# New addresses in a partition for the weights' halves and the attention and convolution outputs of a hybrid decoder layer

## The chip, the core and the metric

The kernel runs on one core of a Trainium2 chip. The metric is the time of one execution on the device, in microseconds (us); the time before is the median of three runs. The engines are called PE (TensorE, matmuls), PEld (its weight loads), DVE (VectorE), ACT (ScalarE), POOL (GpSimd) and SP (SyncE, which here only issues transfers).

## The reference, cut to what matters

One decoder layer, 16 meta tokens and 512 tokens, width 2048, in float32. Each of the four matrix stages below is a product over 2048 or 5632 rows.

```python
n = _rmsnorm(h, g_mix[l])
p = n @ w_in[l]                                   # 2048 x 6144
q, k, v, gb, gc, u = jnp.split(p, ...)
o_attn = _stick_breaking_attention(q, k, v)       # 8 heads of 128
o_conv = gb * _causal_dwconv(gc * u, conv_w[l])   # 1024 channels
o = jnp.concatenate([_rmsnorm(o_attn, ...), _rmsnorm(o_conv, ...)], axis=-1)
h = h + o @ w_out[l]                              # 2048 x 2048
n2 = _rmsnorm(h, g_ffn[l])
h = h + (jax.nn.silu(n2 @ w_gate[l]) * (n2 @ w_up[l])) @ w_down[l]   # 5632 wide
```

The meta tokens' rows are dropped at the end.

## The kernel before

**Split operands.** A float32 product is made of three matmuls in the type fp32r: each operand is split in a high part (a rounded copy) and a low part (what is left), and the sum is high x high + high x low + low x high. So for each tile of 128 rows of the contraction (a k tile, counted by k) there are three matmuls in a row, at lines 168, 170 and 172 in the input projection, 662 to 664 in the output projection (`wide_product`) and 676 to 678 in the feed-forward part (`block_product`). The weights are the stationary operand (128x128), the activations the moving one (512, 264, 258 or 256 columns).

**Stages in order.** (1) Input projection, with attention woven into it head by head, then eight convolution groups; its weight halves `whi`, `wlo` are in the pool wpool. At the end of a head, ACT and DVE write the head's output as two halves, `oah` and `oal` (pool oapool, at the left end of memory); at the end of a convolution group `och` and `ocl` (pool ocpool, right above it). (2) Output projection, 16 tiles of 16 k tiles, 48 matmuls each, moving operands `oa` and `oc` of 512 columns; but for the first tile its weights are split into `s`. (3) Gate and up: 44 pairs, made from seven block products each in place of eight (a scheme that forms sums and differences of quarters of the operands); a block product has 8 k tiles, 24 matmuls of 256 columns. Its moving operands are the seven activation blocks `f0` to `f6` (tiles of the helper `slot`, in pools fpool and fpool_last). (4) Down projection: 32 pairs in four chunks of 5, 6, 5 and 6 k tiles, again seven block products per pair; its moving operands are 12 ring slots (`ring_tile`: `r0` to `r6`, and five slots in the tile `rest`), loaded by POOL from DRAM (`fd`), where stage 3 stored them (line 852).

**Weights in stages 2 to 4.** SP loads quarters into the tiles `b11`, `b12`, `b21`, `b22` (in stage 2 under the name `wide`), DVE forms sums `t1` to `t3`, and `split_quad` (line 591: ACT writes the high part; line 592: DVE the low one) fills one of three tiles `s`, [128, 2, 1024]. All of these are in the pool `sw`, allocated from the right end of memory below the pool hpool, which holds one tile, `acc_h`.

**Order and waits.** Each engine works through its own instructions in the order of the program; a matmul waits by semaphore for the halves that it reads. Pools are stacks from the left or right end of a partition's memory. They are opened with `reuse_waits="tile"`: a tile placed over a released pool waits for the old tiles that it overlaps, each as a whole.

**Addresses before.** All below are bytes modulo 256 within a partition, as they come out of the pools' sizes. `s`, `b`, `t` and `acc_h` start at 224, as `whi` and `wlo` do; `f0` to `f6` and all ring slots start at 240 (`slot` leaves 16 bytes at the front of a tile that starts at 224); `oah`, `oal`, `och` and `ocl` start at 224. The input projection's moving operands `nh` and `nl` start at 224, 32, 96 and 160 in turn, and are read from there, from 1056 bytes on (two halves of 264 columns), from 48 bytes on (258 columns), or from 64 bytes on (512 columns). Within a tile the k tiles follow each other at 512 bytes for weights, and at 1024 bytes for `f` and the rings.

Of the kernel before, what the change touches and what calls it, by code (L numbers as in the profile page):

```python
# [9 lines left out]
F32 = mybir.dt.float32  # L10
F32R = mybir.dt.float32r
# [4 lines left out]
P = 128  # L16
D = 2048
SEQ = 512
# [14 lines left out]
def hybrid_layer(ctx: ExitStack, tc: tile.TileContext, xT, w_in, w_out, w_gu, w_down, vecs, out):  # L33
# [250 lines left out]
    oapool.tile([P, 8], F32, name="pad_oa")  # L284
    acc_c = oapool.tile([P, SEQ], F32, name="acc_c")
    acc_a = oapool.tile([P, SEQ], F32, name="acc_a")
    oa = []

    def halves(ps, n):
# [67 lines left out]
    def attend(h, kn, kh, kl, qn, qh, ql, vt):  # L357
# [98 lines left out]
        def mix(ws):  # L456
            o = small(f"o{h}")
            for b in range(3):
                kk, q0 = slice(b * P, (b + 1) * P), Q0[b]
                th, tl = ws[b]  # L460
                pe.matmul(o[:, q0:], vh[:, kk], th, start=b == 0, stop=False)
                pe.matmul(o[:, q0:], vh[:, kk], tl, start=False, stop=False)
                pe.matmul(o[:, q0:], vl[:, kk], th, start=False, stop=False)
            pe.matmul(o[:, Q0[3] :], v32[:, :P], lw[:, 1184:1328], start=False, stop=False)
            pe.matmul(o[:, Q0[4] :], v32[:16, P:], lw[:16, 1328:1344], start=False, stop=True)
            g = g_att[:, h : h + 1]
            oh = oapool.tile([P, SEQ], F32R, name=f"oah{h}")
            ol = oapool.tile([P, SEQ], F32R, name=f"oal{h}")
            sc.activation(oh, o, AF.Copy, scale=g)
            ve.scalar_tensor_tensor(ol, o, g, oh.bitcast(F32), ALU.mult, ALU.subtract)  # L470
            square_sum(acc_a, o, h == 0)
            oa.append((oh, ol))
# [28 lines left out]
    for j in range(HEADS):  # L501
        pc = pp.tile([P, 2, 512], F32, tag="pp", name=f"pc{j}")
        product([(pc[:, 0, :CH], C0, C0 + CH), (pc[:, 1, :CH], C0 + CH, L)], n_hl)
        cu = t512(2 * CH, "e", 2)[:, : 2 * CH]
        ve.tensor_tensor(two(cu), halves(pc, CH), two(r2[:, C0:]), ALU.mult)
        pu = pp.tile([P, 2, 512], F32, tag="pp", name=f"pu{j}")
        product([(pu[:, 0, :CH], C0, C0 + CH), (pu[:, 1, :CH], C0 + CH, L)], n_hl)
        ve.tensor_tensor(two(cu), halves(pu, CH), two(cu), ALU.mult)
        y = t512(SEQ, "e2", 2)[:, :SEQ]
        sc.activation(y, cu[:, 2 : 2 + SEQ], AF.Copy, scale=cw[:, 3 * j : 3 * j + 1])  # L510
        for t in (1, 2):
            ve.scalar_tensor_tensor(
                y, cu[:, 2 + t : 2 + t + SEQ], cw[:, 3 * j + t : 3 * j + t + 1], y, ALU.mult, ALU.add
            )
        pb = pp.tile([P, 2, 512], F32, tag="pp", name=f"pb{j}")
        product([(pb[:, 0, :], META, L)], n_hl)
        gb = t512(SEQ, "v", 2)[:, :SEQ]
        ve.tensor_tensor(gb, pb[:, 0, :], r[:, META:], ALU.mult)
        gp.tensor_tensor(y, y, gb, ALU.mult)
        g = g_cnv[:, j : j + 1]  # L520
        if j == 0:
            assert not waiting
            after(10, scale_a)
            apool.release()
            ocpool = open_pool("ocpool")
        oh = ocpool.tile([P, SEQ], F32R, name=f"och{j}")
        ol = ocpool.tile([P, SEQ], F32R, name=f"ocl{j}")
        sc.activation(oh, y, AF.Copy, scale=g)
        ve.scalar_tensor_tensor(ol, y, g, oh.bitcast(F32), ALU.mult, ALU.subtract)
        square_sum(acc_c, y, j == 0)  # L530
        oc.append((oh, ol))
# [18 lines left out]
    hpool = open_pool("hpool", side="right")  # L550
    sw = open_pool("sw", side="right")
    acc_h = hpool.tile([P, SEQ], F32, name="acc_h")
    pairs = []
    def gate_up(f):
        return 8, [w_gu[n, f, k] for k in range(2) for n in range(2)]
# [160 lines left out]
    fpool = open_pool("fpool", side="right")  # L716
    hbuf = open_pool("hbuf", side="right")

    def slot(pool, dt, n, tag, name, gap=64):

        t = pool.tile([P, 2 * n * T2 + gap], dt, tag=tag, name=name)
        return t[:, 4 : 4 + 2 * n * T2].rearrange("p (a k t) -> p a k t", a=2, k=n)

    def pad(pool):
        pool.tile([P, 8], F32, name=f"pad_{pool.name}")

    acts = {i: slot(fpool, F32R, 8, f"f{i}", f"f{i}") for i in (0, 1, 2, 5)}
    fx = {i: dram.tile([P, 2, 8, T2], F32R, name=f"fx{i}") for i in (3, 4, 6)}
    for _ in range(4):
        load_wide()  # L730
# [11 lines left out]
    for i, j in enumerate(OUT_TILES):  # L742
# [32 lines left out]
        if i == KT - 1:  # L775
            with tc.high_priority(1 << 20):
                residual(ve)
                square_sum(acc_h, hj, False, wide_tmp("s"))
                mixed_blocks()
            ocpool.release()  # L780
            oapool.release()
            fp = open_pool("fp")
            rings_p = [open_pool("ring_0")]
            pad(rings_p[0])
            rings, n_ring, rest = {}, [0], []

            def ring_tile(dt, name):
                i = n_ring[0] % 12
                n_ring[0] += 1
                if i < 7:  # L790
                    return slot(rings_p[0 if i == 0 else 1 if i < 6 else 2], dt, 6, f"r{i}", name)
                if not rest:
                    rest.append(rings_p[2].tile([P, 5 * 12 * T2 + 16], F32R, name="rest"))
                t = rest[0][:, 4 : 4 + 5 * 12 * T2].rearrange("p (s a k t) -> p s a k t", s=5, a=2, k=6)
                return t[:, i - 7]

            r0 = ring_tile(F32R, "r0_0")
            fpool_last = open_pool("fpool_last")
            for s, n in ((3, 7), (4, 7), (6, 8)):
                acts[s] = slot(fpool_last, F32R, 8, f"f{s}", f"f{s}")  # L800
                for part in range(2):
                    gp.dma_start(acts[s][:, part, :n], fx[s][:, part, :n], max_dma_last_dim=4096)
            split_f(3, 6)
            split_f(4, 7)
        else:
            residual(gp if half else ve)
            if half:
                split_f(5, 2)
                st = hbuf.tile([P, 2, 2, T2], F32R, tag="st", name=f"st{j}")[:, :, 0]
                split(st[:, 0], st[:, 1], src[:, 3])  # L810
                gp.dma_start(fx[6][:, :, k], st)
            else:
                mixed_blocks()
                st = hbuf.tile([P, 2, 2, T2], F32R, tag="st", name=f"st{j}")
                split(st[:, 0], st[:, 1], src[:, 6:8])
                for n, s in enumerate((3, 4)):
                    gp.dma_start(fx[s][:, :, k], st[:, :, n])
# [56 lines left out]
    def load_acts(c, s):  # L874
        if c < len(CHUNKS):
            n = CHUNKS[c]
            rings[c, s] = (ring_tile(F32R, f"r{c}_{s}") if c or s else r0)[:, :, :n]

            for part in range(2):
                gp.dma_start(rings[c, s][:, part], fd[c][s][:, part], max_dma_last_dim=3072)  # L880
# [19 lines left out]
    rings_p.append(open_pool("ring_a", side="right"))  # L900
    for s in range(1, 6):
        load_acts(0, s)
    gate(FT - 1, g1, u1, x)
    apool.release()
    fpool_last.release()
# [3 lines left out]
    for c in range(len(CHUNKS)):  # L909
        end = c == len(CHUNKS) - 1  # L910
        if end:
            hh = ring_tile(F32, "hh")
        for j in range(KT // 2):

            if 1 <= j <= 5:
                load_acts(c + 1, j - 1)
            c1 = cpool.tile([P, 2, T2], F32, tag="c1", name=f"d1_{c}_{j}")
            c2 = cpool.tile([P, 2, T2], F32, tag="c2", name=f"d2_{c}_{j}")
            if end:
                h2 = [hh[:, :, 2 * (j % 3) + m] for m in range(2)]  # L920
                for m in (1, 0):
                    gp.dma_start(h2[m], two(hs[2 * j + m]))
            x = pair_product([rings[c, s] for s in range(7)], c1, c2)
            if j == KT // 2 - 1:
                for s in (5, 6):
                    load_acts(c + 1, s)
            if end:
                gp.tensor_tensor(c2, c2, h2[1], ALU.add)
                gp.tensor_tensor(c2, c2, r_h, ALU.mult)
                nc.sync.dma_start(two(out[2 * j + 1]), c2)  # L930
                ve.tensor_tensor(c1[:, 0], c1[:, 0], h2[0][:, 0], ALU.add)
                ve.tensor_tensor(c1[:, 0], c1[:, 0], r_h[:, 0], ALU.mult)
                ve.tensor_tensor(c1[:, 1], x, h2[0][:, 1], ALU.add)
                ve.tensor_tensor(c1[:, 1], c1[:, 1], r_h[:, 1], ALU.mult)
                nc.sync.dma_start(two(out[2 * j]), c1)
            else:
                sc.copy(c1[:, 1], x)
                gp.dma_start(two(hs[2 * j + 1]), c2, accum_op=ALU.add)
                gp.dma_start(two(hs[2 * j]), c1, accum_op=ALU.add)
# [61 lines left out]
```

## Time and profile before

| | |
|---|---|
| runs, median (lowest to highest) | 2148.52 us (2145.52 to 2150.7) |
| profiled execution, its own time | 2144.11 us |
| its span, first to last instruction | 2142.4 us |
| TensorE's mean granted clock | 0.996 of 2.4 GHz |

Stages in that span: input projection with attention and convolution to 629 us, output projection to 803, gate and up to 1686, down projection to the end. A profile is one execution; "busy" for an engine is time in which an instruction of its own runs, and a matmul's end is modelled, so matmuls overlap in the records and the distance between their starts says more than their durations.

### The profile page before, as it was taken

What the parts mean: (1) busy time and instruction counts of PE and PEld (TensorE: products, weight loads), DVE (VectorE), ACT (ScalarE), POOL (GpSimd) and SP (SyncE); (2) the same over time, 40 slices, a digit from 0 to 9 for tenths busy, and PEclk for the clock granted to TensorE, in tenths of its full rate; (3) what the DMA queues carried; (4) which work ended last, traced back from release to release, by engine and by line L of the source; (5) the groups of instructions that cost most, each with busy time, mean ns of one, the idle gap of its engine ahead of it and who ended that gap; (6) DMA issues with size and microseconds to landing.
All of it is one profiled execution on the core that took longest, in us unless ns stands there. A gap on an engine that the chain in (4) does not pass through costs nothing.

```text
span 2142.4 us, 39382 instructions
## 1 busy us (share of the span) xinstructions
PE 2109.6 (98%) x16086; PEld 2031.4 (95%) x16086; DVE 1644.2 (77%) x2131; ACT 1020.4 (48%) x1576; POOL 458.6 (21%) x584
## 2 busy tenths in 40 slices
PE   8999999999999998999999999999999899999999
PEld 7999999999988888999999999999999899999999
DVE  8777777434337778898888888888889777777798
ACT  6666565322224434554445455445445444444443
POOL 4111111101014453221211211211111323121222
PEclk9999999999999999999999999999999999999999
DMA  5222222232235556555555655655555999788763
GB/s 171 79 80 70 79 78 76 84 99 89 94 127 178 177 163 226 170 176 178 176 168 153 175 166 153 182 158 153 168 152 147 310 261 302 181 248 223 225 186 113
DMA packets 146005, 342.48 MB, mean 160 GB/s; under 512 B 13392, under 2 KB 58960, under 8 KB 145824
## 3 DMA queue, kind: packets, MB, share of 16 engines
q1 hardware_dynamic: 67824, 214.33, 31.6%
q0 software_dynamic: 78000, 125.63, 21.6%
q8 instruction: 126, 2.06, 0.4%
q14 instruction: 55, 0.45, 0.1%
HBM read 268.60 MB, written 71.30 MB: 159 GB/s over the span
## 4 chain that ended last, share of the span: by engine, by line
PE 91%; DMA 4%; DVE 3%; issue 1%; ACT 1%; POOL 0%; SPq 0%; DVEq 0%; ACTq 0%
PE x L676 11%; PE x L678 11%; PE x L677 10%; PE z L676 5%; PE z L678 5%; PE z L677 5%; PE y L678 3%; PE y L677 3%; PE y L676 3%; PE po L662 3%; PE po L663 3%; PE po L664 3%; DMA b<-w_down 2%; PE pv L168 1%; PE pu L172 1%; PE pc L172 1%
## 5 line engine op out<-in xcount | busy, mean ns | idle before, releaser
L591 ACT CAST s<-t 128x1024 fp32r<-128x1024 f32 (+2 forms) x304 | 285.5, 939 | 423.6 <-PE z L678 138.2
L592 DVE TENSOR_TENSOR s<-t,s 128x1024 fp32r<-128x1024 f32 (+2 forms) x304 | 347.0, 1141 | 105.3 <-ACT s L591 103.6
L677 PE MATMUL x<-f,s 128*128 128x256 f32 x1408 | 394.3, 280 | 2.1 <-DVE f L183 1.3
L678 PE MATMUL x<-f,s 128*128 128x256 f32 x1408 | 394.2, 280 | 1.8 <-DVE s L592 1.8
L676 PE MATMUL x<-f,s 128*128 128x256 f32 x1408 | 393.9, 280 | 0.0
L591 ACT CAST s<-b 128x1024 fp32r<-128x1024 f32 (+2 forms) x228 | 214.3, 940 | 243.6 <-PE x L678 236.9
L677 PEld LDWEIGHTS x<-f,s 128*128 128x128 f32 x1408 | 264.9, 188 | 2.5 <-DVE f L183 1.5
L678 PEld LDWEIGHTS x<-f,s 128*128 128x128 f32 x1408 | 265.0, 188 | 2.0 <-DVE s L592 2.0
L676 PEld LDWEIGHTS x<-f,s 128*128 128x128 f32 x1408 | 264.8, 188 | 0.3 <-ACT f L182 0.2
L592 DVE TENSOR_TENSOR s<-b,s 128x1024 fp32r<-128x1024 f32 (+2 forms) x228 | 247.9, 1087 | 5.2 <-ACT s L591 3.5
L137 DVE TENSOR_TENSOR wlo<-raw,whi 128x512 fp32r<-128x512 f32 (+1 forms) x198 | 143.4, 726 | 131.3 <-ACT whi L136 130.7
L852 POOL DMA_DIRECT2D fd<-s x154 | 108.8, 924 | 615.1 <-DVE s L183 613.6
L136 ACT CAST whi<-raw 128x512 fp32r<-128x512 f32 (+1 forms) x198 | 121.3, 614 | 186.2 <-PE pu L170 65.5
L676 PE MATMUL z<-f,s 128*128 128x256 f32 x704 | 197.1, 280 | 0.9 <-ACT p L697 0.9
L677 PE MATMUL z<-f,s 128*128 128x256 f32 x704 | 196.6, 279 | 0.0
L678 PE MATMUL z<-f,s 128*128 128x256 f32 x704 | 196.6, 279 | 0.0
L598 DVE TENSOR_TENSOR t<-b,b 128x1024 f32<-128x1024 f32 (+2 forms) x152 | 166.4, 1094 | 25.3 <-DMA b<-w_down 21.4
L676 PEld LDWEIGHTS z<-f,s 128*128 128x128 f32 x704 | 132.1, 188 | 1.5 <-ACT p L697 1.3
L678 PEld LDWEIGHTS z<-f,s 128*128 128x128 f32 x704 | 132.1, 188 | 0.0
L677 PEld LDWEIGHTS z<-f,s 128*128 128x128 f32 x704 | 132.1, 188 | 0.0
L676 PE MATMUL x<-r,s 128*128 128x256 f32 x424 | 118.7, 280 | 4.2 <-DVE d L705 3.0
L677 PE MATMUL x<-r,s 128*128 128x256 f32 x424 | 118.2, 279 | 2.4 <-DMA r<-fd 2.4
(345 smaller groups left out, 5823.1 us busy)
## 6 DMA issues: line engine op xcount, KB each, us to landing
b<-w_gu SPq DMA_DIRECT2D x176, 512.0 KB, 3.6
raw<-w_in SPq DMA_DIRECT2D x92, 512.0 KB, 3.3
fd<-s POOLq DMA_DIRECT2D x154, 256.0 KB, 5.2
b<-w_down SPq DMA_DIRECT2D x64, 384.0 KB, 4.0
b<-w_down SPq DMA_DIRECT2D x64, 320.0 KB, 4.8
wide<-w_out SPq DMA_DIRECT2D x30, 512.0 KB, 3.7
r<-fd POOLq DMA_DIRECT2D x24, 640.0 KB, 13.1
hd<-d POOLq DMA_DIRECT2D x48, 256.0 KB, 5.6
```

The lines of the kernel that those rows point to most:

```text
L136: sc.copy(hi[:, :c], raw)
L137: ve.tensor_tensor(lo[:, :c], raw, hi[:, :c].bitcast(F32), ALU.subtract)
L591: sc.copy(hi, src)
L592: ve.tensor_tensor(lo, src, hi.bitcast(F32), ALU.subtract)
L598: ve.tensor_tensor(sums[name], a, b, ALU.add)
L662: pe.matmul(ps, hi[:, kk], ah, start=k == 0, stop=False)
L663: pe.matmul(ps, hi[:, kk], al, start=False, stop=False)
L664: pe.matmul(ps, lo[:, kk], ah, start=False, stop=k == 7)
L676: pe.matmul(ps, hi[:, kk], act[:, 0, k], start=start and k == 0, stop=False, skip_group_check=not start)
L677: pe.matmul(ps, hi[:, kk], act[:, 1, k], start=False, stop=False, skip_group_check=not start)
L678: pe.matmul(ps, lo[:, kk], act[:, 0, k], start=False, stop=k == n - 1, skip_group_check=not start)
L852: gp.dma_start(fd[c][s][:, :, k], t[:, :, i])
```

## The change

Weight tiles of the pool sw and the activation tiles are moved to other addresses in a partition; no instruction that computes or moves data is added or taken away.

- hpool gets a 24-float pad, which moves hpool and sw down by 96 bytes: `acc_h`, `b`, `t` and `s` now start at 128 modulo 256.
- fpool and ring_a get a pad of 160 bytes, which puts the `f` blocks and ring slots back to 240. Space for this is found by giving `f0` and `f1` one tile, `f2` and `f5` one tile, ring slots 1 and 2 one tile (`slots`, with one gap of 64 floats per tile instead of one per slot). Ring slots keep their order; the places are listed in `groups`.
- The eight heads' `oah` and `oal` become views of one tile of 8192 + 8 floats, read from its fifth float on: they start at 240. The convolution's become views of one tile behind a pad of 128 bytes, in a pool that now begins at 0 modulo 256: they start at 128.
- Nothing changes in wpool and for the input projection's operands.

The diff, without the parts that only rename:

```diff
+    def o_slots(pool, name, at):
+
+        t = pool.tile([P, 2 * HEADS * SEQ + 8], F32R, name=name)[:, at : at + 2 * HEADS * SEQ]
+        return t.rearrange("p (h a t) -> p h a t", h=HEADS, a=2)
+
+    oa_all = o_slots(oapool, "oa", 4)
...
-            oh = oapool.tile([P, SEQ], F32R, name=f"oah{h}")
-            ol = oapool.tile([P, SEQ], F32R, name=f"oal{h}")
+            oh, ol = oa_all[:, h, 0], oa_all[:, h, 1]
...
             ocpool = open_pool("ocpool")
-        oh = ocpool.tile([P, SEQ], F32R, name=f"och{j}")
-        ol = ocpool.tile([P, SEQ], F32R, name=f"ocl{j}")
+            ocpool.tile([P, 32], F32, name="pad_oc")
+            oc_all = o_slots(ocpool, "oc", 0)
+        oh, ol = oc_all[:, j, 0], oc_all[:, j, 1]
...
     acc_h = hpool.tile([P, SEQ], F32, name="acc_h")
+    hpool.tile([P, 24], F32, name="pad_h")
...
-    def slot(pool, dt, n, tag, name, gap=64):
-
-        t = pool.tile([P, 2 * n * T2 + gap], dt, tag=tag, name=name)
-        return t[:, 4 : 4 + 2 * n * T2].rearrange("p (a k t) -> p a k t", a=2, k=n)
...
+    def slots(pool, dt, m, n, name, **kw):
+
+        c = 2 * m * n * T2
+        t = pool.tile([P, c + 64], dt, name=name, **kw)
+        t = t[:, 4 : 4 + c].rearrange("p (s a k t) -> p s a k t", s=m, a=2, k=n)
+        return [t[:, s] for s in range(m)]
...
-    acts = {i: slot(fpool, F32R, 8, f"f{i}", f"f{i}") for i in (0, 1, 2, 5)}
+    acts = {}
+    for a, b in ((0, 1), (2, 5)):
+        acts[a], acts[b] = slots(fpool, F32R, 2, 8, f"f{a}{b}")
+    pad(fpool, 160)
...
+            groups = {0: (0, 1), 1: (1, 2), 3: (1, 1), 4: (1, 1), 5: (1, 1), 6: (2, 1), 7: (2, 5)}
...
+                if i == len(ring):
+                    p, m = groups[i]
+                    ring.extend(slots(rings_p[p], F32R, m, 6, f"ring{i}", tag=f"ring{i}"))
+                return ring[i]
...
     rings_p.append(open_pool("ring_a", side="right"))
     for s in range(1, 6):
         load_acts(0, s)
+    pad(rings_p[1], 160)
```

## Rows read from the trace of the kernel before

**Rows 1.** The page, first part: busy time, share of the span, instructions.

```profile
PE 2109.6 (98%) x16086; PEld 2031.4 (95%) x16086; DVE 1644.2 (77%) x2131; ACT 1020.4 (48%) x1576; POOL 458.6 (21%) x584
```

**Rows 2.** Table of stretches of the feed-forward part; columns as in its first line.

```profile
core 0: us, PE busy (x) PEld busy (x) DVE busy (x) ACT busy (x) POOL busy (x), PEclk, DMA share, GB/s
842.00:918.00 76.00, 76.00 (x643) 76.00 (x642) 66.89 (x73) 37.22 (x49) 16.13 (x20) 1.00 0.57 167
922.00:954.00 32.00, 32.00 (x284) 32.00 (x284) 28.76 (x31) 15.63 (x19) 6.47 (x9) 1.00 0.63 181
960.00:1434.00 474.00, 474.00 (x3996) 474.00 (x3996) 417.50 (x452) 234.76 (x307) 93.26 (x122) 1.00 0.57 168
1442.00:1680.00 238.00, 238.00 (x2042) 238.00 (x2041) 209.33 (x232) 118.35 (x157) 36.46 (x51) 1.00 0.54 157
1714.00:1740.00 26.00, 24.76 (x210) 24.19 (x208) 18.42 (x27) 12.49 (x24) 9.66 (x12) 1.00 1.10 328
1745.00:1785.00 40.00, 40.00 (x355) 40.00 (x354) 33.02 (x46) 20.90 (x39) 8.79 (x11) 1.00 0.72 168
1810.00:1916.00 106.00, 106.00 (x911) 106.00 (x911) 82.39 (x101) 49.91 (x81) 21.48 (x27) 1.00 0.81 210
...
2030.00:2138.00 108.00, 107.38 (x905) 107.13 (x904) 98.18 (x129) 45.88 (x69) 32.66 (x26) 1.00 0.49 147
```

**Rows 3.** Timeline of PE at 925 and 1000: start, duration, instruction.

```profile
924.88 0.28 PE L676 MATMUL x<-f,s 128*128 128x256 f32 x1
...
925.56 0.28 PE L676 MATMUL y<-f,s 128*128 128x256 f32 x1
...
1000.04 0.28 PE L676 MATMUL z<-f,s 128*128 128x256 f32 x1
...
1000.75 0.28 PE L676 MATMUL z<-f,s 128*128 128x256 f32 x1
```

**Rows 4.** Timelines of PEld and PE behind a stall at 1792.

```profile
1792.00 0.19 PEld L676 LDWEIGHTS x<-r,s 128*128 128x128 f32 x1 [2.02 <-ACT s L591]
1792.11 0.19 PEld L677 LDWEIGHTS x<-r,s 128*128 128x128 f32 x1
...
1792.22 0.28 PE L677 MATMUL x<-r,s 128*128 128x256 f32 x1
1792.34 0.28 PE L678 MATMUL x<-r,s 128*128 128x256 f32 x1
```

**Rows 5.** Table of stretches: output projection, 512 columns.

```profile
660.00:800.00 140.00, 140.00 (x619) 115.99 (x618) 100.67 (x130) 55.23 (x90) 68.25 (x73) 1.00 0.60 179
```

**Rows 6.** Waits of PE for the low parts of s: total us, times, longest.

```profile
PE x L678 <- DVE s L592: 2.1, 2, 1.8
PE y L678 <- DVE s L592: 1.4, 3, 0.7
```

**Rows 7.** Table of stretches: input projection, 258 columns, then 512.

```profile
458.00:480.00 22.00, 22.00 (x184) 22.00 (x184) 7.54 (x10) 5.48 (x9) 2.96 (x2) 1.00 0.27 86
481.00:491.00 10.00, 10.00 (x45) 8.13 (x44) 4.35 (x7) 2.58 (x4) 0.00 (x0) 1.00 0.24 76
```

**Rows 8.** Timeline of POOL, and the chain's matmul, at the end of the output projection.

```profile
802.69 1.53 POOL L802 DMA_DIRECT2D f<-fx  x2
...
809.78 1.45 POOL L802 DMA_DIRECT2D f<-fx  x2
...
802.93 0.24 PE po L664
```

**Rows 9.** Timelines of POOL and PE where the down projection begins.

```profile
1674.27 4.59 POOL L880 DMA_DIRECT2D r<-fd  x6
1682.81 2.85 POOL L880 DMA_DIRECT2D r<-fd  x4 [3.94 <-issue]
...
1688.79 0.39 PE L677 MATMUL x<-r,s 128*128 128x256 f32 x1 [1.14 <-DMA r<-fd]
1692.95 0.39 PE L677 MATMUL z<-r,s 128*128 128x256 f32 x1 [1.73 <-DMA r<-fd]
```

More of the change, by code (lines that the diff above doesn't have):

```diff
@@ L717, in hybrid_layer, with slot, pad @@
     hbuf = open_pool("hbuf", side="right")
-    def slot(pool, dt, n, tag, name, gap=64):
-        t = pool.tile([P, 2 * n * T2 + gap], dt, tag=tag, name=name)
-        return t[:, 4 : 4 + 2 * n * T2].rearrange("p (a k t) -> p a k t", a=2, k=n)
-    def pad(pool):
-        pool.tile([P, 8], F32, name=f"pad_{pool.name}")
-    acts = {i: slot(fpool, F32R, 8, f"f{i}", f"f{i}") for i in (0, 1, 2, 5)}
+    def slots(pool, dt, m, n, name, **kw):
[3 more added lines that the diff above has]
+        return [t[:, s] for s in range(m)]
+    def slot(pool, dt, n, tag, name):
+        return slots(pool, dt, 1, n, name, tag=tag)[0]
+    def pad(pool, n):
+        pool.tile([P, n // 4], F32, name=f"pad_{pool.name}")
+    acts = {}
+    for a, b in ((0, 1), (2, 5)):
+        acts[a], acts[b] = slots(fpool, F32R, 2, 8, f"f{a}{b}")
+    pad(fpool, 160)
     fx = {i: dram.tile([P, 2, 8, T2], F32R, name=f"fx{i}") for i in (3, 4, 6)}
@@ L783, in hybrid_layer, with ring_place @@
             rings_p = [open_pool("ring_0")]
-            pad(rings_p[0])
-            rings, n_ring, rest = {}, [0], []
-            def ring_tile(dt, name):
+            pad(rings_p[0], 32)
+            rings, n_ring, ring = {}, [0], []
+            groups = {0: (0, 1), 1: (1, 2), 3: (1, 1), 4: (1, 1), 5: (1, 1), 6: (2, 1), 7: (2, 5)}
+            def ring_place():
                 i = n_ring[0] % 12
                 n_ring[0] += 1
[L790 to L797, printed above, removed]
+                if i == len(ring):
+                    p, m = groups[i]
+                    ring.extend(slots(rings_p[p], F32R, m, 6, f"ring{i}", tag=f"ring{i}"))
+                return ring[i]
+            r0 = ring_place()
             fpool_last = open_pool("fpool_last")
@@ L876, in load_acts @@
             n = CHUNKS[c]
-            rings[c, s] = (ring_tile(F32R, f"r{c}_{s}") if c or s else r0)[:, :, :n]
+            rings[c, s] = (ring_place() if c or s else r0)[:, :, :n]
             for part in range(2):
@@ L911, in hybrid_layer @@
         if end:
-            hh = ring_tile(F32, "hh")
+            hh = slots(rings_p[1], F32, 1, 6, "hh", tag="ring4")[0]
         for j in range(KT // 2):
```

## The prediction

> **What bounds the kernel now.** The page's first part comes first: TensorE is busy for 98% of the span and its weight loads for 95% [rows 1]. A busy share alone doesn't say that a matmul is as short as it can be, so the next view is the table of stretches of the feed-forward part, each free of long waits [rows 2]. There I divide the length of a stretch by its matmuls (less 2.4, which began before it: 0.28 us of duration over 0.117 us of spacing). The same instruction, 128x128 weights by 256 columns, comes every 118.7 ns in 960 to 1434 (474 / 3993.6), every 118.6 in 842 to 918, every 116.7 in 1442 to 1680 (238 / 2039.6), and in 1810 to 1916, and every 113.5 ns in 922 to 954 and 1745 to 1785. The granted clock is 1.00 (2.4 GHz) in all of them, and TensorE is busy all of the time, so no engine or transfer explains the difference. The timeline shows it matmul by matmul: six steps take 0.68 us at 925 (113.3 ns each) and 0.71 us at 1000 (118 ns) [rows 3]. What the reader is to see: one of three paces holds for hundreds of microseconds and changes only at a stall.
>
> Where TensorE restarts after a wait, the second weight load comes 0.11 us after the first, which had no earlier matmul to wait for; after that loads and matmuls go in step, at 0.11 to 0.12 [rows 4]. So a load needs nearly the whole of a 256-column matmul. In the output projection, where the same weight tiles s feed 512-column matmuls, a load has twice the time, and there the spacing is 140 / 617.3 = 226.8 ns [rows 5], twice 113.4. I read from this that 113.4 ns per 256 columns is what the moving side takes, and that the 3 to 5 ns above it are a load of s that isn't ready in time. That is inferred: no row names the load as the releaser.
>
> **The change part by part.** The layout follows from the pool sizes; addresses here are bytes modulo 256 in a partition. *Weights.* The 24-float pad in hpool moves all of sw down by 96 bytes: s goes from 224 to 128. It is the stationary operand of all feed-forward matmuls (44 x 7 x 8 x 3 = 7392 for gate and up, 8 x 7 x 22 x 3 = 3696 for down, 11,088 in all) and of 720 of the 768 in the output projection. The 160-byte pads bring f and the rings back to 240, where they are now. So in the feed-forward part only the weights' address changes. No instruction is added or removed. What the new address does to a load no row shows. Its bounds are the paces seen: none below 113.4, and the dearest above it stands under the rivals. I take the lower end, because a k tile of s is 512 bytes that from 224 lie across nine 64-byte lengths, and from 128 fill eight whole ones, so that a load touches less; that this counts is a guess. If a load then always finishes under its matmul, every stretch goes to 113.4. The gain by stretch [rows 2], count times excess: 842 to 918, 641 x 5.2 = 3.3 us; 960 to 1434, 3994 x 5.3 = 21.2; 1442 to 1680, 2040 x 3.3 = 6.7; 1714 to 1740, 208 x 3.3 = 0.7; 1810 to 1916, 909 x 3.3 = 3.0; 2030 to 2138, 903 x 5.3 = 4.8; the two fast ones nothing. Sum 39.7 us for 9346 of the 11,088, 4.2 ns each; the other 1742 would give 7.4 at that, of which I take 5.3 since many lie around stalls: 45 us.
>
> What takes some of it back: in 1714 to 1740 the DMA share is 1.10 and TensorE already waits there, so the chunks that begin so get nothing earlier than their transfers; and VectorE, 88% busy in 960 to 1434, would be 92% busy at the faster pace [rows 2]. I give back 4 us: about as much again as TensorE waits today for VectorE's s (2.1 + 1.4) [rows 6]. The ends are 0, and 11: twice those waits and the gains of the two stretches with a DMA share over 0.7 that have one (0.7 + 3.0). Net 41, between 34 and 47 (with all of the 7.4).
>
> A rule of the Trainium skill speaks against this gain. TensorE: Matmul & The Clock Gate, section "Step-by-step: what each phase is for", says that the moving operand and the weight load have read ports of their own, so that loading the next weights takes nothing from the running matmul; by that, no address of s would matter, and the sum would be 2148.5. The three paces of one instruction at one pair of addresses don't look like two independent streams, but they don't disprove the rule.
>
> *Attention and convolution parts.* oa goes from 224 to 240; oc, by the 32-float pad after a pool that now ends at 0, to 128. Both are moving operands of 512 columns, now at the floor (226.8) [rows 5]. So they can only stay or lose. The bound above is the same width in the input projection, where the operands lie at 32, 96, 160 and 224 in turn: 481 to 491 holds 43.3 matmuls in 10 us, 230.9 ns [rows 7], 4.1 above; 768 x 4.1 = 3.2 us. Below, 0. The feed-forward operands at 240 reach the same floor per column, so I take 1 us.
>
> *Merged tiles.* oa, oc, f0 with f1, f2 with f5 and two ring slots become parts of larger tiles; a pool opened over them waits by whole tiles. At the end of the output projection the first load into the old place of oa is issued at 802.69 and the second only at 809.78; the last matmul that reads oc starts at 802.93 [rows 8], so waiting for all of oc moves nothing that is late: 0. At the change to the down projection, ring slot 3 will lie over the tile of f2 and f5, and waits for f5's last read instead of f2's: its two issues leave the first batch (six from 1674.27) and join the second (four from 1682.81) [rows 9]. Behind them on GpSimd's queue stand the issues for slots 4 and 5, two issues of 0.7 us later, while slots 1 and 2 have the transfers to themselves and land earlier. TensorE waits there 1.1 and 1.7 us on such loads [rows 9]; the edit costs between -1.5 and +1.5. I take +1, as the issues behind are late by that much.
>
> Sum on the profiled execution: 2144.1 - 45 + 4 + 1 + 1 = 2105.1. The median of the runs lies 4.4 above that execution, so **2109 us**.
>
> **The rivals.** *Half way:* the pace is chosen anew at each restart [rows 4], and the new address may only shift the choice. If the middle pace (116.7) took the place of the slow one, 641 + 3994 + 903 matmuls would gain 2.0 ns, 11 us; with a third of all at 113.4 and the rest at 116.7 the mean falls from 117.6 (113.4 + 4.2) to 115.6, 22 us: about 2130. *Nothing changes:* the address of the load doesn't count, by the rule above or because the moving side at 240 sets the paces: 2148 to 2150, with the small costs. For it speaks that all three paces occur at the present addresses, so the address alone doesn't fix one. *Slower:* what counts may be the distance between the two streams. It is 16 bytes now and becomes 112. In the input projection, with weights at 224 too, the moving operands lie at many other distances, and 258 columns take 22 / 181.6 us = 121.1 ns [rows 7], where 258/256 of 113.4 would be 114.3: 6.8 above the floor, against 4.2 now in the feed-forward part. If s at 128 brings that, the price is 11,088 x 2.6 = 29 us: 2177. It decides from the point where the new mean spacing is over 117.6. Against it: those operands change their alignment from one matmul to the next, which the feed-forward ones don't.
>
> **How the numbers follow.** Chances: forecast (2109) 0.42, half way 0.18, nothing 0.18, slower 0.22. Under 0.2% (4.3 us) a measurement can't tell a change of this kernel from none: faster 0.60, same 0.18, slower 0.22. For 8 in 10 the range takes in the forecast with its ends (47 us of gain and ring loads 1.5 us better: 2100), the half way and the unchanged case with the upper costs (2148.5 + 3.2 + 1.5, rounded up: 2154), and leaves the slower one out. The likeliest case's own range is 2100 to 2119 (34 us of gain, 3.2 for oa and oc, 1.5 for the ring).
>
> **What would show it.** Right: the stretches of the feed-forward part hold one pace, about 113.4 ns, in gate and up as in down; the output projection keeps 226.8; VectorE's share there rises to 0.92; weight loads stand 113 ns apart. Wrong: stretches at 116.7 or 118.7 remain (half way or nothing), or a new pace above 119 appears with no wait beside it (slower). If the paces fall to 113.4 and the time doesn't, TensorE's waits on VectorE's s or on ring loads will have grown. Longer waits at 1686 to 1706 would show the merged ring tiles; a spacing near 231 in the output projection would show that oa or oc lost their floor.

## The result and the profile after

The changed kernel takes 2111.17 us (median of four runs, 2107.92 to 2112.74) against 2147.02 (2145.14 to 2150.7) for the kernel before, timed beside it: a ratio of 0.983, 95% interval 0.981 to 0.986. The profiled execution of after took 2107.92 us, its span is 2106.2, its mean granted clock 0.998.

The page's first part of after, for [rows 1]:

```profile
PE 2070.5 (98%) x16086; PEld 1987.5 (94%) x16086; DVE 1644.0 (78%) x2131; ACT 1019.5 (48%) x1576; POOL 458.9 (22%) x584
```

TensorE is as full as before, with as many instructions, and 39 us less busy. So nothing was taken off the path; the same matmuls became shorter. The table of stretches of after shows which, for [rows 2] and [rows 5]; the last row is the output projection:

```profile
core 0: us, PE busy (x) PEld busy (x) DVE busy (x) ACT busy (x) POOL busy (x), PEclk, DMA share, GB/s
842.00:874.00 32.00, 32.00 (x285) 32.00 (x284) 28.81 (x32) 16.18 (x21) 7.31 (x10) 1.00 0.63 189
960.00:1434.00 474.00, 472.07 (x4136) 469.85 (x4135) 433.07 (x468) 243.00 (x320) 93.17 (x122) 1.00 0.58 172
1825.00:1875.00 50.00, 50.00 (x444) 50.00 (x443) 40.33 (x48) 24.47 (x40) 8.28 (x11) 1.00 0.70 152
2030.00:2095.00 65.00, 65.00 (x574) 64.90 (x573) 63.46 (x82) 30.61 (x47) 18.85 (x15) 1.00 0.52 162
...
660.00:800.00 140.00, 140.00 (x611) 114.29 (x611) 99.23 (x129) 53.84 (x86) 67.71 (x71) 1.00 0.59 179
```

Worked as in the prediction (busy time over matmuls less 2.4), the feed-forward stretches hold 113.2 (32 / 282.6), 114.2 (restarts included), 113.2 and 113.7 ns, where [rows 2] had 116.7 and 118.7 over most of their length. The timeline of PE says the same; six steps take 0.68 us, 113.3 ns each, as in the fast stretch of [rows 3]:

```profile
919.99 0.28 PE L684 MATMUL x<-f,s 128*128 128x256 f32 x1
...
920.67 0.28 PE L684 MATMUL x<-f,s 128*128 128x256 f32 x1
```

The output projection went the other way, from 226.8 to 229.8 ns (140 / 609.3). The starts of all matmuls of both traces give the account below, in us from the start of the span. "Steady" steps are start-to-start times under 1.2 times the median; the longer ones are priced by what they have over 113.4 ns.

| | before | after | difference |
|---|---|---|---|
| start of the output projection | 628.4 | 627.3 | -1.1 |
| output projection | 174.6 | 177.0 | +2.4 |
| gate and up | 880.8 | 852.5 | -28.3 |
| down projection, to the start of its last matmul | 454.4 | 445.2 | -9.2 |
| of the last two: steady steps, excess over 113.4 ns | 10,989 x 4.02 = 44.1 | 10,972 x 0.12 = 1.4 | -42.8 |
| of the last two: 98 and 115 long steps | 33.8 | 39.1 | +5.3 |

The last two rows add to -37.5, as the two stages do; with the first two rows that makes the span's -36.2. The -1.1 is within what executions differ by: over the traces of all runs below, the output projection starts between 627.1 and 628.6.

What grew is at stalls. Part of the long steps is TensorE's clock: among the stalls of the feed-forward part the granted clock fell to 0.50 (1.2 GHz), twice before and once after, and there steps of some 214 ns stand in a row, 30 of them before (3.0 us) and 13 after (1.3 us). The two stretches of before, then the one of after:

```profile
828.00:831.00 3.00, 3.00 (x16) 3.00 (x15) 2.97 (x2) 0.00 (x0) 2.14 (x1) 0.50 0.43 164
2016.00:2019.00 3.00, 3.00 (x16) 3.00 (x15) 2.50 (x4) 1.10 (x2) 1.38 (x4) 0.50 1.05 308
```

```profile
1663.50:1665.50 2.00, 2.00 (x11) 2.00 (x11) 2.00 (x2) 0.47 (x1) 0.00 (x0) 0.50 1.22 392
```

Without these the stalls grew by 7.0 us. Waits of PE in gate and up: before (860 to 1670), then after (860 to 1640); total us, times, longest:

```profile
PE z L676 <- ACT p L697: 0.3, 1, 0.3
```

```profile
PE z L684 <- ACT p L705: 2.4, 9, 0.3
```

An accumulator z whose old content ScalarE hasn't copied out yet now holds TensorE up nine times in this record, where it had done so once. By the starts of the matmuls, with the slow step after each restart counted too, it is 16 stalls against 3, and 6.9 us of long steps against 0.8 (7.5 in the changed kernel's second trace, e12_again). The waits for the weight halves s grew as well. Over the whole span, those for VectorE's low parts went from 3.9 us (2.1 and 1.4 [rows 6], and 0.4) to 5.5 (3.2 and 1.9 below, and 0.4; 4.5 in the second trace), and those for ScalarE's high parts are new:

```profile
PE y L686 <- DVE s L600: 3.2, 4, 1.4
PE x L684 <- ACT s L599: 2.4, 3, 0.9
PE x L686 <- DVE s L600: 1.9, 2, 1.5
```

### The profile page after: what moved, and what is told of

Its sections match the earlier page's. It is cut to its first block, busy times and chain, and to the rows that moved or that the text cites. A ratio compares the mean times of both kernels' runs of the same rounds, so it can differ in the third digit from the quotient of the medians.

```text
span 2106.2 us, 39382 instructions
## 1 busy us (share of the span) xinstructions
PE 2070.5 (98%) x16086; PEld 1987.5 (94%) x16086; DVE 1644.0 (78%) x2131; ACT 1019.5 (48%) x1576; POOL 458.9 (22%) x584
## 4 chain that ended last, share of the span: by engine, by line
PE 87%; DVE 5%; DMA 4%; issue 2%; ACT 1%; POOL 0%; SPq 0%; DVEq 0%; ACTq 0%
PE x L684 10%; PE x L686 9%; PE x L685 9%; PE z L684 5%; PE z L685 5%; PE z L686 5%; PE y L686 3%; PE y L685 3%; PE y L684 3%; PE po L671 3%; PE po L670 3%; PE po L672 3%; DMA b<-w_down 2%; DVE s L600 2%; PE pv L168 2%
## 5 line engine op out<-in xcount | busy, mean ns | idle before, releaser
L686 PE MATMUL x<-f,s 128*128 128x256 f32 x1408 | 387.3, 275 | 1.5 <-DVE s L600 1.5
L685 PE MATMUL x<-f,s 128*128 128x256 f32 x1408 | 387.4, 275 | 1.3 <-DVE f L183 1.3
L684 PE MATMUL x<-f,s 128*128 128x256 f32 x1408 | 387.3, 275 | 0.2 <-ACT f L182 0.2
L684 PE MATMUL x<-ring,s 128*128 128x256 f32 x704 | 195.7, 278 | 8.6 <-DVE d L713 5.6
L684 PE MATMUL z<-f,s 128*128 128x256 f32 x704 | 195.8, 278 | 3.3 <-ACT p L705 3.1
L685 PE MATMUL x<-ring,s 128*128 128x256 f32 x704 | 194.8, 277 | 3.3 <-DMA ring<-fd 3.3
L686 PE MATMUL x<-ring,s 128*128 128x256 f32 x704 | 195.0, 277 | 0.4 <-DVE s L600 0.4
L686 PE MATMUL z<-f,s 128*128 128x256 f32 x704 | 193.9, 275 | 0.0
L685 PE MATMUL z<-f,s 128*128 128x256 f32 x704 | 193.9, 275 | 0.0
L684 PEld LDWEIGHTS x<-ring,s 128*128 128x128 f32 x704 | 132.7, 189 | 10.7 <-issue 8.5
L684 PEld LDWEIGHTS z<-f,s 128*128 128x128 f32 x704 | 132.1, 188 | 6.5 <-ACT p L705 6.3
```

The source lines that it names most:

```text
L684: pe.matmul(ps, hi[:, kk], act[:, 0, k], start=start and k == 0, stop=False, skip_group_check=not start)
L685: pe.matmul(ps, hi[:, kk], act[:, 1, k], start=False, stop=False, skip_group_check=not start)
L686: pe.matmul(ps, lo[:, kk], act[:, 0, k], start=False, stop=k == n - 1, skip_group_check=not start)
```

## The experiments

All are edits of the changed kernel. "Distance" means the start of the moving operand less the start of the weights s, modulo 256 bytes. In the feed-forward part it was 16 before (240 - 224) and is 112 after (240 - 128); in the output projection it was 0 (224 - 224), and after it is 112 for oa and 0 for oc. Three theories stood at the outset. **A:** s is better at 128 by its own alignment (the prediction's guess). **B:** the distance decides. **C:** the merged tiles, not the addresses, bring the gain.

**The weights back at 224, all else as changed.**

```diff
-    hpool.tile([P, 24], F32, name="pad_h")
...
-    pad(fpool, 160)
+    pad(fpool, 256)
...
-    pad(rings_p[1], 160)
+    pad(rings_p[1], 256)
```

> The changed kernel with the weights' tiles s back at 224 modulo 256; f, rings, oa, oc and the merged tiles stay as changed. Theory (the weights' address does it): the feed-forward spacing goes back to a mix of 113, 117 and 119 ns, mean about 117.5, and the time to 2145 to 2150 us. Rival (the merged tiles or their waits brought the gain): the spacing stays at 113.4 and the time near 2111. In the output projection, oa at 240 or oc at 128 with weights at 224: 227 if the moving address alone sets the pace there and 240 is as good as 224, 231 if not.

Measured: 2150.32 us (2139.01 to 2156.54, ten runs), ratio to the kernel before 1.0012 (0.9993 to 1.0032). Its table of stretches has the old paces back: 119.1, 114.0, 118.8 and 116.7 ns.

```profile
842.00:918.00 76.00, 75.61 (x637) 75.61 (x638) 66.85 (x74) 37.74 (x51) 15.25 (x20) 1.00 0.55 164
922.00:954.00 32.00, 32.00 (x283) 31.93 (x282) 28.76 (x33) 16.14 (x21) 5.53 (x8) 1.00 0.59 175
960.00:1434.00 474.00, 473.75 (x3991) 473.48 (x3990) 417.70 (x452) 234.93 (x308) 93.07 (x121) 1.00 0.57 169
1442.00:1640.00 198.00, 198.00 (x1699) 198.00 (x1699) 173.69 (x193) 99.10 (x131) 27.67 (x39) 1.00 0.55 160
```

C falls: with merged tiles and s at 224 the feed-forward part takes 1332.8 us, against 1335.2 before and 1297.7 after. (oa and oc stay at 240 and 128 here, and beside s at 224 the output projection takes 179.3 us, 4.7 more than before.) The pair f at 240, s at 224 gives three paces again, in the order of [rows 2].

**The attention and convolution outputs at 224, the weights at 128.**

```diff
-        t = pool.tile([P, 2 * HEADS * SEQ + 8], F32R, name=name)[:, at : at + 2 * HEADS * SEQ]
+        t = pool.tile([P, 2 * HEADS * SEQ], F32R, name=name)[:, at : at + 2 * HEADS * SEQ]
...
-    oa_all = o_slots(oapool, "oa", 4)
+    oa_all = o_slots(oapool, "oa", 0)
...
-            ocpool.tile([P, 32], F32, name="pad_oc")
```

> The changed kernel with oa and oc both at 224 modulo 256, as before; s stays at 128. Feed-forward part as in the changed kernel (113.4 ns, near 2111 us). Output projection: if the pair of addresses counts only through the weights, 227 ns per 512 columns and 2.2 us gained against the changed kernel (360 x 4.0 + 360 x 2.0 ns); if 224 needs weights at 224 to be at the floor, it stays at 229 to 231.

Measured: 2116.49 us (2112.97 to 2118.23, four runs), ratio 0.985 (0.983 to 0.987). The output projection takes 179.4 us and 233.3 ns per matmul (from start to start), where the same 224 gave 226.8 beside weights at 224:

```profile
660.00:800.00 140.00, 140.00 (x602) 112.62 (x601) 97.05 (x129) 53.75 (x86) 65.60 (x70) 1.00 0.58 177
```

One address of the moving operand is good beside one address of s and bad beside another. The feed-forward part stays at 113.5.

**A against B: the weights at 160, and at 192.** Both have the blocks f at one distance and the ring slots at another. The diff is that of s at 160; for s at 192 the pads are 8 floats and 224 bytes, and `at` is 4 for f and 20 for the rings.

```diff
-    hpool.tile([P, 24], F32, name="pad_h")
+    hpool.tile([P, 16], F32, name="pad_h")
...
-        t = t[:, 4 : 4 + c].rearrange("p (s a k t) -> p s a k t", s=m, a=2, k=n)
+        at = 12 if n == 8 else 4
+        t = t[:, at : at + c].rearrange("p (s a k t) -> p s a k t", s=m, a=2, k=n)
...
-    pad(fpool, 160)
+    pad(fpool, 192)
...
-    pad(rings_p[1], 160)
+    pad(rings_p[1], 192)
```

> s at 160; f at 16 (112 bytes beyond s, as in the changed kernel), rings at 240 (80 beyond s). Theory A (what counts is that s starts on a 64-byte multiple): both stages show paces above 113.4, mean 116 to 119, about 2148 us. Theory B (what counts is the distance of 112 bytes from weights to moving operand): gate and up stay at 113.4 ns and only the down projection gets slower, by up to 3696 x 4 ns = 15 us, 2111 to 2126 us.

> s at 192; f at 240 (48 bytes beyond s), rings at 48 (112 beyond s). Theory A (s on a 64-byte multiple): both stages at 113.4 ns, about 2111 us. Theory B (distance of 112): gate and up above 113.4, by 2 to 5 ns on 7392 matmuls (15 to 37 us: 2126 to 2148 us), the down projection at 113.4. If it must be a 128-byte multiple, both are above.

Measured: 2125.97 us with s at 160, f at 16 (distance 112), rings at 240 (distance 80); 2140.4 us with s at 192, f at 240 (distance 48), rings at 48 (distance 112). One stretch of gate and up and one of the down projection, for s at 160, then 192:

```profile
960.00:1434.00 474.00, 471.61 (x4132) 469.40 (x4131) 432.92 (x466) 241.71 (x319) 94.84 (x122) 1.00 0.58 173
1825.00:1870.00 45.00, 45.00 (x377) 45.00 (x376) 34.80 (x42) 20.60 (x33) 5.12 (x6) 1.00 0.65 141
```

```profile
960.00:1434.00 474.00, 474.00 (x4007) 473.91 (x4006) 418.73 (x454) 235.90 (x310) 93.26 (x121) 1.00 0.57 169
1825.00:1870.00 45.00, 44.88 (x395) 44.72 (x394) 36.51 (x46) 21.31 (x35) 6.06 (x7) 1.00 0.72 188
```

With one s at 160, f runs at the floor (114.2 with restarts, 113.5 for steady steps) and the rings at 120; with one s at 192 it is the rings that are near it (114.3, steady 113.8) and f at 118.4. Whichever stage has distance 112 is fast, at three addresses of s (128, 160, 192) and three of the moving operand (240, 16, 48). A falls; B holds.

**The other distances.** Four kernels with s at 128 put f and the rings elsewhere by the first index of the view alone. The diff is that of the first (distances 0 and 128); the others have `at` at 12 and 20 (144 and 176), 36 and 0 (240 and 96), 2 and 6 (104 and 120):

```diff
-        t = t[:, 4 : 4 + c].rearrange("p (s a k t) -> p s a k t", s=m, a=2, k=n)
+        at = 40 if n == 8 else 8
+        t = t[:, at : at + c].rearrange("p (s a k t) -> p s a k t", s=m, a=2, k=n)
```

> s at 128 as in the changed kernel; f at 128 (0 bytes beyond s), rings at 0 (128 beyond s). Theory B (the distance decides, and 112 is special): at 0 gate and up at 116 to 120 ns, at 128 the down projection above 113.4 unless the good distances reach on from 112. Rival A' (any moving address that is not 240 or 48 beyond is fine once s is right): both at 113.4, 2111 us. By B the time is 2130 to 2165 us.

> s at 128; f at 16 (144 beyond s), rings at 48 (176 beyond s). Theory B, with a window of good distances around 112: 144 near 113.4 or just above, 176 above. Without any window: both between 116 and 120 ns, 2140 to 2165 us. e3 and e4 gave 119.5 at 80 and 118.3 at 48.

> s at 128; f at 112 (240 beyond s, that is 112 + 128), rings at 224 (96 beyond). If the good distances recur every 128 bytes, gate and up run at 113.4 ns. If 112 stands alone in 256 bytes, 116 to 120, as at 0, 16, 48, 80, 128, 144 and 176. Rings at 96: 113.4 if the good distances begin 16 bytes ahead of 112, above 116 if not. Time 2111 (both good) to 2160 us (none).

> s at 128; f at 232 (104 beyond s, off a 16-byte multiple), rings at 248 (120 beyond). If the good stretch is wider than 8 bytes on a side and a start off a 16-byte multiple costs nothing, both stay at 113.4. In the input projection the starts off a 16-byte multiple (24, 88, 152, 216) ran 3 to 4 ns above their neighbours, so by that row 116 to 118 in both, 2135 to 2155 us.

Measured: 2161.38, 2154.09, 2146.24 and 2173.87 us (one run each; the kernel before gave 2148.67 beside the first two, 2144.79 beside the others). The same two stretches of each, in this order:

```profile
960.00:1434.00 474.00, 474.00 (x3952) 474.00 (x3951) 413.88 (x448) 232.64 (x304) 94.45 (x120) 1.00 0.55 166
1825.00:1870.00 45.00, 45.00 (x381) 45.00 (x381) 34.76 (x43) 20.80 (x33) 6.96 (x9) 1.00 0.82 219
```

```profile
960.00:1434.00 474.00, 473.96 (x4013) 473.45 (x4012) 419.91 (x455) 236.19 (x310) 93.07 (x122) 1.00 0.57 170
1825.00:1870.00 45.00, 45.00 (x380) 45.00 (x379) 35.53 (x44) 20.78 (x33) 5.20 (x6) 1.00 0.77 185
```

```profile
960.00:1434.00 474.00, 474.00 (x4036) 472.95 (x4036) 422.58 (x457) 237.25 (x313) 96.43 (x122) 1.00 0.58 170
1825.00:1870.00 45.00, 45.00 (x378) 45.00 (x376) 34.70 (x42) 20.41 (x33) 5.12 (x6) 1.00 0.64 138
```

```profile
960.00:1434.00 474.00, 474.00 (x3952) 474.00 (x3951) 414.99 (x450) 233.90 (x306) 92.30 (x120) 1.00 0.56 164
1825.00:1870.00 45.00, 45.00 (x371) 45.00 (x370) 34.30 (x42) 20.02 (x32) 8.29 (x10) 1.00 0.93 262
```

No other distance comes near 112. Means of the steady steps of all runs, in ns; only 16 and 112 were seen in both stages, 0, 48, 104, 144 and 240 in gate and up alone, the rest in the down projection alone, each in one execution:

| distance | 0 | 16 | 48 | 80 | 96 | 104 | **112** | 120 | 128 | 144 | 176 | 240 |
|---|---|---|---|---|---|---|---|---|---|---|---|---|
| 256 columns | 120.0 | 116.6 to 117.8 | 118.3 | 119.6 | 120.0 | 120.0 | **113.5 to 113.8** | 121.7 | 118.7 | 118.2 | 119.3 | 117.1 |

Eight bytes to either side cost 6 to 8 ns of 113.5; the two starts there, 232 and 248, are also the only ones tried that aren't multiples of 16, so part of that price may be theirs. The neighbours at multiples of 16, at 96 and 128, cost 6.5 and 5.2. The good place doesn't come back after 128 bytes (240 is 112 + 128), but it does after 256: the tile of f0 and f1 is 33,024 bytes long, so the blocks of the next tile, f2 and f5, lie 256 bytes further modulo 512, and in the changed kernel gate and up is at the floor throughout. A plain story, such as streams that collide when they are close, doesn't give this shape. In the kernel at 104 and 120 the changed kernel's gain turns into a loss: 29 us above the kernel before (2173.87 - 2144.79).

**What the two streams do to each other.** If a load of s that is late sets the pace, a load of half the columns should give the floor at any distance. Two kernels, with s at 224 (distance 16) and at 128 (distance 112), halve every matmul but the first of a block: 128 of 256 moving columns in gate and up, 64 of 128 weight columns in the down projection. The edit, to which the first adds that of the weights back at 224:

```diff
+            w, m = (P, T2 // 2) if n == 8 else (P // 2, T2)
+            ww, mm = (P, T2) if k == 0 else (w, m)
...
-            pe.matmul(ps, hi[:, kk], act[:, 1, k], start=False, stop=False, skip_group_check=not start)
+            pe.matmul(ps[:w, :m], hi[:, kk][:, :w], act[:, 1, k, :m], start=False, stop=False, skip_group_check=True)
```

> s at 224, f and rings at 240 (distance 16, as before the change). Left out: in gate and up all but the first matmul of a block takes only 128 of the 256 columns (weights whole); in the down projection all but the first loads only 64 of the 128 weight columns (256 moving columns). Theory L (the weight load, stretched by the address, is what is late): gate and up, where nothing but the load can limit, come at 109 to 118 ns, more than in e8; the down projection, with a load of half the length, at 113.4 (no more 117 or 119). Rival M (the load's reads hold up the moving stream): gate and up at 108 as in e8, the down projection still above 113.4, at 115 to 119. The time itself tells nothing.

> The same with s at 128 (distance 112); the same work left out: all but the first matmul of a block has 128 columns in gate and up, and 64 weight columns in the down projection. Theory L: gate and up at 108 ns (a load undisturbed), less than in e7; down at 113.4. Rival M: both as in e7 for gate and up, down at 113.4. If the load of s from 128 is shorter only because of its own address, gate and up differ from e7 by more than 2 ns.

Measured: 2840.38 and 2843.08 us, both longer than a kernel with twice the columns. The tables of stretches say why; s at 224, then 128:

```profile
806.00:812.00 6.00, 5.07 (x43) 4.82 (x41) 5.25 (x8) 2.64 (x5) 1.38 (x3) 1.00 0.99 307
812.00:818.00 6.00, 1.12 (x3) 0.83 (x3) 5.59 (x9) 2.79 (x6) 3.42 (x4) 0.61 1.10 398
818.00:824.00 6.00, 5.92 (x27) 5.83 (x27) 3.60 (x5) 2.35 (x4) 3.10 (x5) 0.50 0.88 278
...
1100.00:1500.00 400.00, 400.00 (x1877) 400.00 (x1876) 200.06 (x215) 111.14 (x147) 50.91 (x62) 0.50 0.33 97
2500.00:2838.00 338.00, 329.09 (x2821) 326.88 (x2819) 274.16 (x360) 154.64 (x251) 82.30 (x89) 1.00 0.74 211
```

```profile
1100.00:1500.00 400.00, 400.00 (x1876) 400.00 (x1877) 199.07 (x212) 111.63 (x148) 49.62 (x62) 0.50 0.33 98
2500.00:2838.00 338.00, 331.93 (x2817) 329.45 (x2815) 275.23 (x360) 154.25 (x251) 80.94 (x87) 1.00 0.74 208
```

In gate and up the granted clock fell to 0.50 (1.2 GHz) at the stall behind the output projection, and stayed there to the end of the stage while matmuls of 128 columns ran, 213.4 ns apart in both (400 / 1874.6). At that clock 256 columns had taken no longer: some 214 ns in the kernel before, from 828 to 831. So there the moving columns don't set the pace, and the distance doesn't show. Ahead of the fall both kernels have some 36 such steps at full clock. The timeline of PE, s at 224, then 128; 18 steps take 2.01 us in both, 111.7 ns each:

```profile
806.88 0.27 PE L686 MATMUL y<-f,s 128*128 128x128 f32 x1
...
808.89 0.28 PE L686 MATMUL y<-f,s 128*128 128x128 f32 x1
```

```profile
804.44 0.27 PE L686 MATMUL y<-f,s 128*128 128x128 f32 x1
...
806.45 0.27 PE L686 MATMUL y<-f,s 128*128 128x128 f32 x1
```

With half a moving stream beside it, a full load comes every 111.7 ns at either distance, a little under the 113.4 of a full matmul. So the prediction's guess that a load is slower from 224 than from 128 doesn't hold in these steps.

In the down projection (clock 1.00) the loads are indeed shorter, 0.13 us against 0.19 for the full one that begins a block, as the timeline of PEld with s at 128 shows:

```profile
2701.06 0.19 PEld L686 LDWEIGHTS x<-ring,s 128*128 128x128 f32 x1
...
2701.30 0.13 PEld L688 LDWEIGHTS x<-ring,s 128*64 128x64 f32 x1
```

But the matmuls don't follow: steady steps of 116.2 ns with s at 224, and 117.1 at the distance that gave 113.5 with full loads. Both kernels hold several paces there: of stretches of twelve matmuls without a stall, 48 of 282 are near 113 ns with s at 224 and most others near 117; with s at 128 it is 17 of 276, and the others run from 116 to 120. If the matmuls only waited for a late load, one that is 0.06 us shorter would bring the floor. It doesn't, so the prediction's late load falls. That 112 is a good distance only for full loads fits two streams that hinder each other in a pattern that depends on both; but that theory, too, had expected about 113.4 with s at 128. How they hinder each other stays open.

**Both outputs of the first stage at distance 0.**

```diff
+    oapool.tile([P, 40], F32, name="pad_oa_all")
-    oa_all = o_slots(oapool, "oa", 4)
+    oa_all = o_slots(oapool, "oa", 0)
...
-            ocpool.tile([P, 32], F32, name="pad_oc")
```

(and `o_slots` without its `+ 8`, as above). The changed kernel itself ran beside it once more.

> The changed kernel with oa too at 128 modulo 256, so that both oa and oc lie 0 bytes beyond s in the output projection. Before the change the pair 224 and 224 ran 227 ns per 512 columns, and so does 128 and 128 after some matmuls. Theory (the distance decides, and 0 is the good one for 512 columns): all 720 at 226.8, 360 x 3.9 + 360 x 1.9 ns = 2.1 us less than the changed kernel, 2109 us. Rival (oa's own address): 229 to 231 stays, 2111.

> The changed kernel once more, beside e9 on the same chip: 2108 to 2113 us; output projection 231 for oa and 229 for oc, feed-forward part 113.5 ns.

Measured: 2112.43 us (2112.31 to 2115.36, four runs), ratio 0.986 (0.984 to 0.988), against 2112.16 (2110.0 to 2115.58, four runs), 0.986 (0.983 to 0.989), for the changed kernel. The output projection is back at 226.7 ns (from start to start) and 174.9 us:

```profile
660.00:800.00 140.00, 140.00 (x620) 115.95 (x619) 100.60 (x131) 55.61 (x90) 68.98 (x73) 1.00 0.59 181
```

The 2.1 us saved there don't show in the total: this trace has 141 long steps in the feed-forward part worth 45.4 us, the repeated one 129 worth 42.0, and the profiled one of after 115 worth 39.1. Between executions of one kernel that differs by 2.9 us, more than the saving. So the stage's gain is shown; one of the whole kernel isn't.

For 512 columns the map over all runs (the 720 matmuls with weights in s, stalls left out) is: distance **0: 226.7** (at 224 and at 128), 16: 231.6, 48: 232.9, 80: 231.1, 96: 233.3, 112: 230.7, 160: 234.1, 192: 233.5, 224: 233.3 ns. The good distance is another than for 256 columns.

## Why the prediction was right, and where its reasons were not

The forecast was 2109 us and the time is 2111; by its own sum 2105.1 for a profiled execution that took 2107.9. The terms held, but the reason under the largest one didn't. The 2.8 us between are small errors that partly cancel: 2.2 less gain, 1.3 more taken back, 1.4 more for oa and oc, less the 1 for the merged tiles and the 1.1 of an early start. (The sums come out, but for the 9346 matmuls, which count those that began before a stretch; without them it is 9329, and nothing hangs on it.)

**Three paces at one pair of addresses** [rows 2, 3]: right, and the reading that carried the forecast. They return with s at 224, and none but the fast one is left at distance 112. The observation that all three occur at the present addresses was held against any effect of the address; what the runs show is that an address pair can leave room for several paces (16) or for one (112).

**The gain of 45 us:** measured 42.8. The step that failed is the reason given for it. The guess that s at 128 fills whole 64-byte lengths, and that a late load makes the excess [rows 4, 5], is refuted: s at 128 gave 117 to 122 ns at eight distances, s at 160 and 192 gave 113.5 and 113.8 at the right one, full loads came every 111.7 ns with s at 224 as at 128, and shorter loads didn't bring the floor. What acts is the distance, the mechanism of the *slower* rival. That rival had it right that 16 becomes 112 and that the distance counts; it took the price from operands at many distances [rows 7], and 112 happens to be the only good one of the twelve tried. Had the activations lain 8 bytes off, the rival's 2177 would have been close (2173.87 measured with 104 and 120). The prediction took the low end of its bounds for a reason that is wrong. That the change lands on the one good distance, and so the sign of the forecast, was luck.

**The rule of the Trainium skill** (TensorE: Matmul & The Clock Gate, section "Step-by-step: what each phase is for") is that the two operands have independent read ports, so that a load takes nothing from the running matmul. What the prediction drew from it, that no address of s would matter, doesn't agree with these runs: the same loads and matmuls take 113.5 or 121.7 ns by the distance between their operands. Whether the reads themselves get in each other's way no run shows.

**What takes some back, 4 us:** measured 5.3; the stalls alone grew by 7.0, and 1.7 less went to steps at the low clock. VectorE's share rose as foreseen (433.07 / 474 = 0.91, from 0.88), but the waits on it carry the lesser part: they grew by 1.6 us (0.6 in the second trace) where the prediction doubled them, and the stalls for z, which wait for ScalarE's copy, by 6.0 (above). The faster pace found the next engine, though not the one named.

**oa and oc, +1 us:** measured 2.4, inside the bound of 3.2. The step that failed is "The feed-forward operands at 240 reach the same floor per column, so I take 1 us": the floor at 240 belonged to 256 columns. The timeline of PE where oa ends and oc begins shows a step of its own:

```profile
664.40 0.39 PE L670 MATMUL po<-oa,s 128*128 128x512 f32 x1
...
666.48 0.40 PE L670 MATMUL po<-oc,s 128*128 128x512 f32 x1
...
669.02 0.39 PE L672 MATMUL po<-oc,s 128*128 128x512 f32 x1
...
671.75 0.39 PE L672 MATMUL po<-oc,s 128*128 128x512 f32 x1
```

oa (distance 112) takes 2.08 us for nine steps, 231 ns; oc (distance 0) begins at 231 (2.54 / 11) and settles at 227 (2.73 / 12). So a stretch inherits its pace from what ran before it and, where the distance is good, runs into the floor by itself. A restart in the feed-forward part of after does the same: over 31 of them the first six steps behind the last long one average 118.3 ns, the next six 115.5, and from the thirteenth on it is 113.3.

**Merged tiles, +1 us:** the waits moved as described, the cost is about nothing. Timeline of POOL, for [rows 9]:

```profile
1647.78 3.09 POOL L896 DMA_DIRECT2D ring<-fd  x4
1654.53 1.42 POOL L896 DMA_DIRECT2D ring<-fd  x2 [3.66 <-PE y L686]
1656.74 2.85 POOL L896 DMA_DIRECT2D ring<-fd  x4 [0.79 <-issue]
```

Six issues became four, and slot 3's two wait 3.66 us for f5's last reader, the y at line 686. TensorE's waits for ring loads there went from 4.4 us to 3.9 (before, 1680 to 1706; then after, 1640 to 1680):

```profile
PE x L677 <- DMA r<-fd: 2.4, 2, 1.2
PE z L677 <- DMA r<-fd: 1.7, 1, 1.7
PE y L676 <- DMA r<-fd: 0.3, 1, 0.3
```

```profile
PE x L685 <- DMA ring<-fd: 3.3, 2, 2.1
PE z L685 <- DMA ring<-fd: 0.6, 1, 0.6
```

**Half way and nothing changes** are excluded by the table after: no stretch at 116.7 or above is left.

## What to carry to other kernels

Where matmuls stand back to back, divide the length of stretches without waits by their count, for each kind of instruction: a kernel at 98% busy still had 4 ns of 117 in each, and a pace that changes only at stalls was the sign. On a kernel with a weight load per matmul, treat the distance between the start of the moving operand and that of the weights, modulo 256 bytes, as something to tune: try the multiples of 16 bytes (both good distances here are such, and their neighbours 16 bytes off, where tried, were bad), for each operand width anew, and move both operands together when an edit shifts a pool. The input projection here still reads its operands at several residues (121.1 ns for 258 columns, 230.9 for 512 [rows 7]); moving them wasn't tried.

## What the runs showed of the hardware

- The time of an fp32r matmul of 256 columns with a load of its own depends on the distance of its two operands: 113.5 ns at 112 bytes modulo 256, 117 to 122 on average at eleven others. With 512 columns the one good distance of nine is 0, 226.7 ns against 231 to 234. Why these two was not settled.
- With 128 moving columns, an fp32r matmul with a full load comes every 111.7 ns at distance 16 and at 112, at full clock.
- At distance 16 three paces (113.5, 116.7, 118.7 ns) hold until the next stall; at 112, and at 0 with 512 columns, the matmuls run into the floor within about a dozen.
- Weight loads of 64 columns take 0.13 us instead of 0.19 without bringing a 256-column matmul to the floor (116.2 and 117.1 ns at distances 16 and 112).
- Halving the moving columns made gate and up longer: the granted clock stood at 0.50 from the first stall to the end of the stage, and the spacing was 213.4 ns, the same as for 256 columns at that clock.
